# Two DMA issues of the first stage change queues: mixed outputs to ScalarE's, w_mod loads to GpSimd's

## The chip, the cores and the metric

The kernel is one program on one core of a Trainium2 chip. The metric is device time in microseconds (us), taken as the median of several runs. The core has five engines, each with an instruction queue of its own that runs in order: TensorE (PE, matmuls, with a separate queue for weight loads, PEld), VectorE (DVE), ScalarE (ACT), GpSimd (POOL) and SyncE (SP, which only issues DMAs). DMAs may be issued from SyncE's, ScalarE's and GpSimd's queues; 16 DMA engines carry them all. An instruction that has to wait for another engine holds everything behind it in its own queue.

## The reference

Two blocks run over 512 tokens of width 1024. The first block is an RWKV/GLA mixer followed by a routed expert layer. The second block has two layers, each a mixer followed by an expert-choice layer, and each modulated by vectors that come from a conditioning row:

```python
mix = jnp.concatenate([y_rw, y_gla], axis=-1)   # y_rw: rwkv7_mixer, y_gla: gla_mixer
x = x + mix @ w_out[l]
x = x + hier_moe(rmsnorm(x, ln2_w[l]), ...)
# second block, per layer l: 6 chunks of 1024
m = jax.nn.silu(c) @ w_mod[l] + b_mod[l]        # w_mod[l]: 1024 x 6144
sh1, sc1, g1, sh2, sc2, g2 = chunks of m
xl = xl + g1 * mixer(modulate(rmsnorm(xl), sh1, sc1))
xl = xl + g2 * ec_moe(modulate(rmsnorm(xl), sh2, sc2), ...)
```

The products with `w_mod` depend on the inputs alone, not on x, so they can run at any time before the second block needs them.

## The kernel before

Three stages follow each other: `phase1` with its expert layer `moe1`, `mixer0` with `moe2`, and `mixer1` with `moe2` again. The change touches `phase1`, the first 606 us.

`phase1` (line 238) norms and transposes x into `hT`. It then computes the recurrent half in four head pairs (`rwkv_pair`, line 359) and the GLA half in two (`gla`, line 620, a generator that yields between steps). Weights are loaded from SyncE's queue by `load` (line 248, DMA at line 251), each into one of two buffers of its kind (`w4` for w_rw; `wb` for w_gl, w_qk, w_v and w_og). Each of the eight 128-row slices of the mixed output is copied out of PSUM by ScalarE and stored to a DRAM buffer `ymix` by `mixed` (line 616), for the recurrent half as `t`, for the GLA half as `gt`. The next stage loads `ymix` again (`yin`, line 834) to multiply by w_out, whose pieces are loaded at line 774 (`st`).

The modulation is a filler. `adaln_block` (line 899) does one of 12 blocks (two layers, six chunks): eight loads of w_mod of 128 x 1024 (512 KB) into two buffers `wm`, four matmuls for each load into one bank `ad` (line 907). For the two gate chunks of a layer GpSimd loads four pieces of the bias `b_gate` (line 914), VectorE adds them (line 917), and GpSimd stores four pieces to `gates` (line 918). For the other chunks ScalarE copies the rows (line 920), TensorE turns them (line 923) and VectorE writes `mods` (line 931). GpSimd's queue also carries `nwr`, the norm weights of each GLA half (line 645), and at the stage's start some constants.

The code calls the fillers between the pairs:

```python
self.rwkv_pair(0, **X); gl(3); fill(6)
self.rwkv_pair(1, **X); gl(6); fill(2)
self.rwkv_pair(2, **X)
self.rwkv_pair(3, **X); fill(3); gl(99); fill(99)
```

This order is a priority, not the order on the chip: the framework plans the whole program when it is built, simulating engines and queues with costs of its own, and puts instructions on each queue as they become ready in that plan. It also adds all waits.

Of the kernel before, what the change touches and what calls it, by code (L numbers as in the profile page):

```python
# [20 lines left out]
T, D = 512, 1024  # L21
# [158 lines left out]
class Kern:  # L180
# [434 lines left out]

    def mixed(self, o, k, ps):
        self.nc.scalar.copy(o, ps)
        self.nc.sync.dma_start(self.ymix[k], o)

    def gla(self, P, bank, S, load, project, hT, gla_gw2, mask, keep, **_):  # L620
        nc, c, V, ident, A = self.nc, self.col, self.nc.vector, self.ident, self.A
# [277 lines left out]
    def adaln_block(self, l, j, w4, bank, row):  # L899

        nc, c = self.nc, self.col
        ps = bank()
        for k in range(KT):
            w = w4()
            nc.sync.dma_start(w, self.A["w_mod"][l, 128 * k:128 * k + 128, D * j:D * j + D])
            for g in range(4):
                nc.tensor.matmul(ps[32 * g:32 * g + 32, 0:256], self.sc[:, k], w[:, 256 * g:256 * g + 256], start=k == 0,  # L907
                                 stop=k == KT - 1, tile_position=(0, 32 * g))
        rows = row()
        if j in (2, 5):  # L910
            q = 2 * l + (j == 5)
            b = row()
            for g in range(4):
                nc.gpsimd.dma_start(b[32 * g:32 * g + 1], self.A["b_gate"][q:q + 1, 256 * g:256 * g + 256])
            for g in range(4):
                z = slice(32 * g, 32 * g + 1)
                nc.vector.tensor_add(rows[z], b[z], ps[z, 0:256])
                nc.gpsimd.dma_start(self.gates[q:q + 1, 256 * g:256 * g + 256], rows[z])
            return
        nc.scalar.copy(rows, ps[:, 0:256])  # L920
        ps = bank()[:, 0:16].rearrange("p (a g m) -> p a g m", a=2, m=2)
        for a in range(2):
            nc.tensor.matmul(ps[:, a], rows[:, 128 * a:128 * a + 128], self.sel, start=True, stop=True)

        where = {0: 1, 1: 0, 3: 3, 4: 2}[j] + 6 * l
        todo = [(where, 0)]
        if l == 0 and j < 2:
            todo.append((4 + (j == 0), 1))
        for slot, m in todo:
            o = self.mods[:, slot]  # L930
            nc.vector.tensor_add(o.rearrange("p (g a) -> p a g", a=2), ps[:, :, :, m],
                                 c(f"b_mod{l}{j}", 0, 8).rearrange("p (g a) -> p a g", a=2))
            if j in (1, 4):
                n = c(f"norm{1 if j == 1 else 2}_g_2{l}", 0, 8)
                nc.vector.scalar_tensor_tensor(o, o, 1.0, n, op0=OP.add, op1=OP.mult)
# [1093 lines left out]
```

## Time and profile before

| | |
|---|---|
| time, median of 3 runs | 2888.31 us (2879.37, 2888.31, 2890.34) |
| profiled execution | 2891.01 us, span of its trace 2889.4 us |
| granted TensorE clock, mean | 0.921 |
| TensorE busy | 2454.6 us (85%) |
| VectorE busy | 1124.1 us (39%) |
| ScalarE busy | 643.5 us (22%) |
| GpSimd busy | 107.0 us (4%) |
| moved by DMA | 778.42 MB, 269 GB/s |

The span is that of the trace; the execution's own time is a little longer. Busy shares are means over stages with different limits, so the first stage has to be read by itself. In the rows, `PE` is TensorE's matmuls and `PEld` its weight loads, `SPq`, `ACTq` and `POOLq` the DMA issues of a queue, `L907` a line of the kernel, and `ad<-wm,sc` a result with its operands. `out <- releaser` names a wait and what ended it.

### The profile page before, as it was taken

The page shows a single profiled execution, that of the slowest core. Times are in us where ns is not written, and L with a number is a line of the kernel's source. Part 1 is how long each engine was busy: PE and PEld are TensorE (multiplying, and loading weights), DVE is VectorE, ACT ScalarE, POOL GpSimd, SP SyncE. Part 2 cuts the span into 40 slices and gives each one's busy share as a digit, 9 for nine tenths or more (in the row PEclk, how much of TensorE's full clock was granted, in tenths as well). Part 3 has the DMA queues.
Part 4 walks back from the last instruction along what each step waited for, and adds up shares of the span by engine and source line. Part 5 has one row for each costly group of instructions (what it writes and reads, how often), then busy time and mean ns, then how long its engine had stood idle before and what let it go on. Part 6 is the DMA issues. An engine that isn't in the chain of part 4 may idle for free. (4 is left out here: it accounts for less than half of the span.)

```text
span 2889.4 us, 36529 instructions
## 1 busy us (share of the span) xinstructions
PE 2454.6 (85%) x15158; PEld 1352.8 (47%) x15158; DVE 1124.1 (39%) x2143; ACT 643.5 (22%) x1049; POOL 107.0 (4%) x193
## 2 busy tenths in 40 slices
PE   7999998775999988868889688988989669888897
PEld 3565655663534544436567433333347553333343
DVE  3867767534121320015875411111239641211112
ACT  3223313221102430005721200010034321000001
POOL 1000000001110000010000000000000000000000
PEclk9999998776999999988899798999999779999999
DMA  4355343056998999983133599999954259999996
GB/s 150 121 174 171 108 129 124 18 187 251 396 367 328 397 393 398 396 346 124 59 124 135 208 409 386 392 406 405 409 195 132 104 203 362 399 405 405 400 409 252
DMA packets 244551, 778.42 MB, mean 269 GB/s; under 512 B 15963, under 2 KB 17243, under 8 KB 243488
## 3 DMA queue, kind: packets, MB, share of 16 engines
q1 hardware_dynamic: 223616, 711.77, 65.2%
q0 software_dynamic: 12448, 41.50, 3.7%
q10 hardware_dynamic: 8320, 22.80, 2.2%
q8 instruction: 120, 1.97, 0.3%
q14 instruction: 47, 0.39, 0.0%
HBM read 748.73 MB, written 27.28 MB: 269 GB/s over the span
## 5 line engine op out<-in xcount | busy, mean ns | idle before, releaser
L1493 PE MATMUL G<-w,xT 128*64 128x256 f32 (+1 forms) x4096 | 772.4, 507 | 22.5 <-DMA w<-in_moe_w_up_dram 18.1
L1493 PEld LDWEIGHTS G<-w,xT 128*64 128x64 f32 x4096 | 293.1, 140 | 380.2 <-issue 287.6
L1513 PE MATMUL Y<-w,hT 128*64 128x512 f32 x1536 | 402.7, 602 | 2.6 <-DMA w<-in_moe_w_down_dram 1.3
L1513 PEld LDWEIGHTS Y<-w,hT 128*64 128x64 f32 x1536 | 172.2, 137 | 195.3 <-issue 182.6
L1498 DVE TENSOR_TENSOR h<-h,G 128x256 f32<-128x256 f32 (+1 forms) x64 | 35.4, 553 | 516.8 <-PE G L1493 406.8
L1761 DVE TENSOR_TENSOR xres<-xres,cb 128x512 f32<-128x512 f32 x116 | 79.6, 687 | 115.4 <-PE cb L1759 115.4
L1750 DVE SCALAR_TENSOR_TENSOR y<-Y,gate,g 128x512 f32<-128x512 f32 x32 | 24.0, 751 | 233.9 <-PE Y L1513 232.3
L321 PE MATMUL mm<-hT,w 128*128 128x512 f32 x240 | 113.2, 611 | 0.0
L1716 PE MATMUL gat<-ident,xg 128*128 128x128 f32 x128 | 30.4, 371 | 95.4 <-DMA xg<-xrow,tok 95.3
L1497 ACT ACTIVATE h<-G 128x256 f32<-128x256 f32 (+1 forms) x64 | 31.4, 491 | 343.3 <-PE G L1493 337.6
L1504 ACT COPY hT<-tr 128x256 f32<-128x256 f32 (+1 forms) x64 | 30.7, 479 | 274.8 <-PE tr L1503 274.8
L907 PE MATMUL ad<-wm,sc 128*32 128x256 f32 x768 | 70.5, 410 | 20.5 <-DMA wm<-in_w_mod_dram 19.1
L1209 PE MATMUL b<-big,wh 128*128 128x512 f32 x320 | 84.2, 415 | 4.4 <-ACT wh L854 3.0
L1751 ACT CAST yhi<-y 128x512 fp32r<-128x512 f32 x30 | 18.6, 619 | 310.5 <-DVE y L1750 224.2
L1716 PEld LDWEIGHTS gat<-ident,xg 128*128 128x128 f32 x128 | 19.1, 183 | 117.9 <-DMA xg<-xrow,tok 88.2
L1209 PEld LDWEIGHTS b<-big,wh 128*128 128x128 f32 x320 | 63.0, 199 | 22.6 <-ACT big L1190 5.4
L1759 PEld LDWEIGHTS cb<-yhi,ohT 128*128 128x128 f32 x114 | 21.4, 188 | 105.2 <-DVE xres L1761 56.8
L1503 PE MATMUL tr<-ident,h 128*128 128x128 f32 x192 | 35.8, 297 | 39.1 <-DVE h L1498 39.0
L636 PE MATMUL g<-wb,hT 128*64 128x128 f32 x1024 | 65.5, 276 | 3.3 <-DVE ga L711 2.6
L321 PEld LDWEIGHTS mm<-hT,w 128*128 128x128 f32 x240 | 42.9, 190 | 51.3 <-issue 50.3
L1759 PE MATMUL cb<-yhi,ohT 128*128 128x512 f32 x114 | 57.5, 504 | 9.7 <-ACT yhi L1751 9.7
L1711 POOL DMA_INDIRECT xg<-xrow,tok x32 | 31.1, 972 | 887.6 <-DVE tok L1793 435.7
(677 smaller groups left out, 3564.7 us busy)
## 6 DMA issues: line engine op xcount, KB each, us to landing
w<-in_exp_w_dram SPq DMA_DIRECT2D x384, 1024.0 KB, 13.2
w<-in_moe_w_gate_dram SPq DMA_DIRECT2D x64, 1024.0 KB, 15.6
w<-in_moe_w_up_dram SPq DMA_DIRECT2D x64, 1024.0 KB, 15.0
w<-in_moe_w_down_dram SPq DMA_DIRECT2D x64, 1024.0 KB, 15.3
wm<-in_w_mod_dram SPq DMA_DIRECT2D x96, 512.0 KB, 4.2
ws<-in_w_in_dram SPq DMA_DIRECT2D x20, 512.0 KB, 4.1
ws<-in_cf_w_dram SPq DMA_DIRECT2D x20, 512.0 KB, 3.5
st<-in_w_out_dram SPq DMA_DIRECT2D x16, 512.0 KB, 4.1
```

Source lines behind the costliest of these rows:

```text
L321: nc.tensor.matmul(ps[:m], w[:, k, col0:col0 + m], hT[:, k], start=k == 0, stop=k == KT - 1)
L636: nc.tensor.matmul(ps[half[h], b], hT[:, k, 64 * j:64 * j + 64], w[h][:, k], start=k == 0, stop=k == KT - 1)
L907: nc.tensor.matmul(ps[32 * g:32 * g + 32, 0:256], self.sc[:, k], w[:, 256 * g:256 * g + 256], start=k == 0, stop=k == KT - 1, tile_positio ...
L1209: nc.tensor.matmul(ps, a[:, k], b[:, k], start=m == 0 and k == 0, stop=m == 2 and k == KT - 1)
L1493: nc.tensor.matmul(parts[m][64 * c:64 * c + 64], xT[:, k, 64 * e:64 * e + 64], w[:, kk, H * c:H * c + H], start=k == 0, stop=k == KT - 1)
L1497: nc.scalar.activation(h, parts[0], AF.Silu)
L1498: nc.vector.tensor_mul(h, h, parts[1])
L1503: nc.tensor.transpose(ps[:, j].rearrange("p c s -> p (c s)"), h[:, 128 * j:128 * j + 128], self.ident)
L1513: nc.tensor.matmul(ys[n][64 * e:64 * e + 64], hTs[e][:, f], ws[e][:, ff_, 512 * n:512 * n + 512], start=f == 0, stop=f == nf - 1)
L1716: nc.tensor.transpose(ps[:, k], xg[:, 512 * b + 128 * k:512 * b + 128 * k + 128], self.ident[:m, :m])
L1759: nc.tensor.matmul(ps, ohT[:m, 128 * t:128 * t + 128], p[k][:m], start=k == 0, stop=k == 1)
L1761: V.tensor_add(xr, xr, ps)
```

## The change

The stores of `mixed` are issued from ScalarE's queue, behind the copy that fills them, and the loads of w_mod from GpSimd's queue. Both were on SyncE's. Sizes, buffers and the computation stay the same. `adaln_block` is called 12 times and `mixed` 8 times, all in the first stage.

```diff
@@ mixed
         self.nc.scalar.copy(o, ps)
-        self.nc.sync.dma_start(self.ymix[k], o)
+        self.nc.scalar.dma_start(self.ymix[k], o)
@@ adaln_block
             w = w4()
-            nc.sync.dma_start(w, self.A["w_mod"][l, 128 * k:128 * k + 128, D * j:D * j + D])
+            nc.gpsimd.dma_start(w, self.A["w_mod"][l, 128 * k:128 * k + 128, D * j:D * j + D])
```

## Rows read from the trace of the kernel before

**Rows 1.** The chain that ended last, its earliest long piece: start, us, what.
```profile
2651.80 0.95 DMA xg<-xrow,tok
```

**Rows 2.** Five stretches: length, busy PE, PEld, DVE, ACT, POOL (instructions), PEclk, DMA share, GB/s.
```profile
17.00:176.00 159.00, 153.77 (x1282) 84.56 (x1282) 96.44 (x189) 42.82 (x70) 1.97 (x4) 1.00 0.36 117
176.00:275.00 99.00, 89.56 (x972) 49.07 (x964) 76.76 (x150) 33.68 (x54) 5.78 (x12) 0.97 0.63 200
275.00:440.00 165.00, 160.61 (x2120) 109.32 (x2120) 112.18 (x244) 49.90 (x87) 4.93 (x10) 0.98 0.37 117
440.00:512.00 72.00, 54.70 (x628) 38.58 (x626) 59.40 (x123) 26.15 (x41) 1.92 (x4) 0.82 0.36 118
512.00:606.00 94.00, 66.74 (x1040) 59.90 (x1040) 39.81 (x90) 18.04 (x31) 1.95 (x4) 0.74 0.03 9
```

**Rows 3.** TensorE's waits, 17.3:440 and 440:607: us in total, times, longest.
```profile
PE ad L907 <- DMA wm<-in_w_mod_dram: 8.5, 12, 1.3
...
PE ad L907 <- DMA wm<-in_w_mod_dram: 10.6, 7, 3.8
```

**Rows 4.** Waits of TensorE's weight loads, 17:606.
```profile
PEld ad L907 <- DMA wm<-in_w_mod_dram: 34.9, 32, 4.3
```

**Rows 5.** Lines L905, L877, L918: duration in ns, min/median/max.
```profile
L905 SPq DMA_DIRECT2D wm<-in_w_mod_dram x96: 327/328/1899, 6.0 to 504.4; - x96
...
L877 POOL DMA_DIRECT2D xrow<-w x12: 533/546/616, 649.9 to 2350.6; - x12
...
L918 POOL DMA_DIRECT2D gates<-rows x16: 487/487/487, 184.5 to 525.0; - x16
```

**Rows 6.** Waits at the head of SyncE's queue, 0:640.
```profile
SPq L905 <- PE ad L907: 202.9, 79, 30.4
```

**Rows 7.** Timeline of SyncE's queue, 484:512: start, us, instruction.
```profile
487.10 0.80 SPq L251 DMA_DIRECT2D wb<-in_w_og_dram  x2
489.70 15.01 SPq L905 DMA_DIRECT2D wm<-in_w_mod_dram  x6
```

**Rows 8.** Timelines of ScalarE and SyncE at the stage's end, 604:611.
```profile
604.20 0.59 ACT L617 COPY gt<-g 128x512 f32<-128x512 f32 x1 [3.76 <-PE g L763]
607.22 0.41 ACTq L1213 DMA_DIRECT2D lnrow<-in_ln_row_dram  x1
...
604.81 0.32 SPq L618 DMA_DIRECT2D ymix<-gt  x1
```

**Rows 9.** DMA issues by line: count, KB each, median us to landing.
```profile
wm<-in_w_mod_dram SPq DMA_DIRECT2D x96, 512.0 KB, 4.2
...
xrow<-w POOLq DMA_DIRECT2D x12, 512.0 KB, 3.0
...
out_dram<-o SPq DMA_DIRECT2D x4, 512.0 KB, 2.7
...
rw_w<-in_rw_w_dram POOLq DMA_DIRECT2D x1, 256.0 KB, 6.1
...
nwr<-in_gla_nw_dram POOLq DMA_DIRECT2D x4, 32.0 KB, 6.9
```

**Rows 10.** Timeline of TensorE, 17:26.
```profile
21.06 1.06 PE L907 MATMUL ad<-wm,sc 128*32 128x256 f32 x2
```

**Rows 11.** The page's costliest groups: busy, mean ns, idle before.
```profile
L907 PE MATMUL ad<-wm,sc 128*32 128x256 f32 x768 | 70.5, 410 | 20.5 <-DMA wm<-in_w_mod_dram 19.1
```

**Rows 12.** Waits of GpSimd's queue, 0:640.
```profile
POOL gates L918 <- DVE rows L917: 254.4, 7, 75.6
...
POOL nwr L645 <- DVE ga L756: 69.5, 1, 69.5
```

**Rows 13.** Timeline of GpSimd, 510:526, the first and last of four.
```profile
513.57 0.49 POOL L918 DMA_DIRECT2D gates<-rows  x1 [69.00 <-DVE rows L917]
...
525.05 0.49 POOL L918 DMA_DIRECT2D gates<-rows  x1 [0.69 <-DVE rows L917]
```

**Rows 14.** Groups of VectorE, 17:606: busy, mean ns.
```profile
L411 DVE TENSOR_TENSOR t<-t,k 128x512 f32<-128x512 f32 x8 | 5.5, 685 | 0.0
```

## The prediction

> **What bounds the kernel now.** The time before is 2888.3 us (median of three, 2879.4 to 2890.3). The profiled execution took 2891.0 us, its trace spans 2889.4 us, so the sum below is made against 2891.0 and 2.7 us are taken off at the end. A measurement of this kernel can tell about 0.5% (14 us) from no change.
>
> I read the chain that ended last first. Its pieces lie in the expert layers near the end of the span [rows 1], and it is silent on the first stage, which runs to about 606 us. For an earlier stage the question is whether its own last instruction comes earlier; the engines' busy time in stretches answers that. From 17 to 176 us and from 275 to 440 us TensorE is busy 153.77 of 159 and 160.61 of 165 us: matmuls, in their order, are the bound. From 176 to 275 us it is busy 89.56 of 99. From 440 to 512 us VectorE is the fuller one (59.40 of 72 us against 54.70), and after 512 us neither is full: dependences between engines set the pace [rows 2]. TensorE runs its instructions in order, so where it is full a late operand pushes back all the rest; where it is not, a late operand can be swallowed.
>
> Then the waits that the change can touch. TensorE's matmul queue waited for a w_mod load 12 times before 440 us, 8.5 us in all, and 7 times after, 10.6 us in all [rows 3]: 19.1 us. Its weight-load queue shows 32 such waits, 34.9 us, most of them beside running matmuls [rows 4]. No engine's list of waits names another load of SyncE's line in this stretch. So 19.1 us, 0.66% of the time, is all that a better w_mod feed can give back directly, and the 8.5 us are the surer part.
>
> **SyncE's side.** It sheds 96 loads at 0.328 us of issue [rows 5], 31 us of queue time, and eight stores. SyncE's line often stands still with a w_mod load at its head, 202.9 us waiting for TensorE to free one of the two buffers [rows 6], and at times with a store there. Neither costs the kernel anything now, because the loads behind them are not missed by anyone. Gone, they free nobody: 0. What can gain is a w_mod load that stands behind another load. The clearest place is 487.10 us, where two w_og loads go out right before the w_mod loads of 489.70 us [rows 7], and the longest wait of TensorE for such a load, 3.8 us [rows 3], falls there. A line of its own would send that load earlier, though the same data engines would still carry three transfers. I take 4 us for all such places; the bounds are 0 and the whole 19.1 us.
>
> **ScalarE's side.** It gains eight issues. A DMA issued from its queue took 0.41 us; the store that SyncE issues now starts at 604.81 us, when the copy (604.20 plus 0.59) has just ended [rows 8]. So a store holds ScalarE for about 0.4 us, eight for 3.3 us, on an engine busy 171 of 589 us [rows 2], which hides them. If all lay on the path they would cost 3.3 us; the last one lies there, and against SyncE's 0.32 us it costs 0.1 us. I take 0.5 us. Behind the last store stand the first issues of the next stage, which wait for its landing anyway.
>
> **GpSimd's side: the turnaround.** With two buffers, load k+2 can go out only when TensorE has read load k. So the dense stretch from 176 us on is paced by the turnaround: buffer free, issue, landing (median 4.2 us [rows 9]). What GpSimd adds to a 512 KB load isn't in this trace; the nearest rows are its 512 KB stores of xrow. They take 0.546 us to issue against SyncE's 0.328 [rows 5] and land in 3.0 us against 2.7 us for SyncE's 512 KB output stores [rows 9]. Depending on whether landing already holds the issue, a turnaround grows by 0.3 us or by 0.5 us. Loads from GpSimd's line show more: nwr landed in 6.9 us and the 256 KB of rw_w in 6.1 us [rows 9], but nwr is made of 512-byte rows, and rw_w went out among the first nine loads of SyncE. I take 0.3, from the row with the same size and row length. On the 19 waits of the matmul queue that is 5.7 us. Upper bound: 6.9 in place of 4.2 us on all 19, 51 us. Below zero I see no reason, since both lines feed the same data engines.
>
> **GpSimd's side: its line.** 96 issues of 0.55 us are 53 us on an engine busy 17 us in 589 [rows 2]; there is room. But the line is in order, and the loads now share it with the gate blocks: four groups of four tiny b_gate loads, four groups of four gate stores at 0.487 us each [rows 5], 1.95 us a group. A w_mod load caught behind a group is that much later. Five of the eight groups lie in or beside the stretches in which TensorE waits for loads now; I take 1 us for three of them, 3 us. Bounds: 0, and 8 times 1.95, 16 us.
>
> The rows of the gate stores also weigh a rule. Their issue is 0.487 us from the shortest to the longest [rows 5], while VectorE is busy two thirds of the time: no issue was held by VectorE. The Trainium skill, "SBUF — State Buffer", section "SBUF: two separate sides" (its "DVE blocks DMA" box), says that GpSimd cannot write DMA descriptors while VectorE runs an operation in a two-port mode, and puts such a transfer at about 3.1 us in place of 0.62. By that figure, 19 exposed loads would lose 2.5 us each, 47 us, for a time of about 2938 us, an estimate from that page. By the row it is 0. The stores measured are of one row each, so a load of 128 rows isn't settled by them; its case stands below as a rival, priced from rows.
>
> **The sum.** 0 + 0.5 + 5.7 + 3 - 4 = +5 us: 2896 us as profiled, 2893 us against the median. The terms' own bounds reach from -19 us to +70 us (3.3 + 51 + 16).
>
> **What the sum can't hold: the order.** The instructions aren't in the order of the code. w_mod matmuls run at 21.06 us [rows 10], before the first recurrent pair, though the code asks for them after it: a planner lays out every queue when the program is built. Moving 96 loads to another queue moves w_mod blocks and all that is packed around them. That can pull either way, and is in the first two rivals.
>
> **Rivals.**
> *Faster: the feed stops stalling TensorE, and blocks slide to where it is idle.* For: a load on its own line can go out as soon as its buffer is free, and TensorE has 17 us and 27 us idle after 440 and 512 us [rows 2]. A w_mod load costs TensorE 70.5 us / 96 = 0.73 us [rows 11]; the last load goes out at 504.4 us [rows 5], 100 us before the stage ends, so blocks may slide. All 19.1 us of waits gone gives 2869 us; ten loads sliding out of the full stretches give 7 us more, 2862. Against: in the dense stretch the loads wait for buffers, not for the queue, and a new queue has no more buffers. Time: 2866 us.
> *Slower: GpSimd's line blocks.* A w_mod load that the planner put behind a gate store waits until VectorE has added the bias, and VectorE runs late. GpSimd stood 254.4 us waiting for VectorE before gate stores and 69.5 us before the nwr load [rows 12], harmless today since nothing stood behind. The last four gate stores went out one by one from 513.57 to 525.05 us [rows 13], 12 us in place of 2. If two blocks in the full stretches do that with loads behind, the cost is 2 x 10 us; with the turnaround's 5.7 us that is 2914 us. It decides from the point where TensorE waits longer than the 3.8 us of today for one load. Against: the planner knows the wait and may put the next two loads ahead of it.
> *Slower: GpSimd's loads land late.* If they land as rw_w did, 1.9 us later than now, the 19 waits grow by 36 us: with the sum's other terms about 2923 us. One way to it is VectorE holding the issue: half an operation (0.685 us for a 512-wide one [rows 14]) for the 65% of the time that VectorE is busy is 0.22 us a load, on 19 to 96 loads 4 to 21 us, 2897 to 2914 us. I put the case at 2915. Against: the flat 0.487 us, and the 3.0 us of the xrow stores.
> *The change does nothing, because buffers and not queues pace the loads,* is the ground of the forecast itself and has no time of its own.
>
> **Numbers.** Forecast (2879 to 2902 us) 0.46; faster rival 0.26; blocked line 0.19; late landing 0.09. Faster by over 0.5% (below 2874): 0.25; within 0.5%: 0.48, which takes a little of each rival; slower (above 2903): 0.27. The range runs from the faster rival's 2862 us to 2922 us, past both slower rivals' times; what lies beyond, towards the sum's upper bound, is less than 2 in 10.
>
> **What would show it.** Right: TensorE's waits for w_mod loads in the first stage stay within 12 to 35 us, w_mod issues from GpSimd at about 0.55 us, landing within 0.5 us of 4.2, the stage ends within 10 us of 606. SyncE's heads shrink and nobody notices. ScalarE's stores start within 0.1 us of their copies' ends. Wrong: landings above 6 us or issues of uneven length (late landing, VectorE's hold); a single wait over 4 us with GpSimd stopped before a gate store or nwr (the blocked line); waits gone, or the first stage ending more than 15 us early with w_mod matmuls past 510 us (the slide). A stage end that moves with w_mod waits unchanged would say that the new order, not the queue's speed, made the difference.

## The result, and the profile after

The changed kernel takes 2912.59 us (median of 8 runs, 2902.82 to 2919.68) against 2889.39 us for the kernel before (8 runs beside it): ratio 1.0078, 95% interval 1.0059 to 1.0097. Measured again beside the experiments it gave 1.0072 (1.0059 to 1.0085). It is slower by about 22 us, 0.75%, where +5 us was forecast as the likeliest. The time lies inside the forecast range. It is also near the 2914 us of the rival in which GpSimd's line blocks, but it came about in another way: that nearness is luck.

The profiled execution spans 2911.5 us. Its five stretches, to be held against [rows 2] (the same columns: length, busy PE, PEld, DVE, ACT, POOL, PEclk, DMA share, GB/s):

```profile
17.00:176.00 159.00, 153.09 (x1238) 83.88 (x1240) 96.49 (x189) 41.33 (x67) 12.54 (x24) 0.99 0.36 115
176.00:275.00 99.00, 85.46 (x872) 46.47 (x872) 71.93 (x142) 29.87 (x48) 22.81 (x44) 0.98 0.63 197
275.00:440.00 165.00, 156.08 (x2101) 105.69 (x2102) 110.79 (x242) 49.96 (x86) 17.96 (x34) 0.96 0.33 106
440.00:512.00 72.00, 58.52 (x692) 41.87 (x687) 56.37 (x118) 25.78 (x44) 10.40 (x20) 0.84 0.39 126
512.00:606.00 94.00, 68.28 (x1106) 57.34 (x1106) 44.94 (x101) 18.72 (x31) 3.01 (x6) 0.74 0.07 23
```

TensorE is 4 us less busy from 176 to 275 us and 4.5 us less from 275 to 440 us: it stands still in the very stretches that it paces. What it stands for is in the lists of waits, matmul queue and weight-load queue, 17 to 640 us (us in total, times, longest; before: [rows 3, 4]):

```profile
PE ad L907 <- DMA wm<-in_w_mod_dram: 33.7, 28, 6.5
...
PEld ad L907 <- DMA wm<-in_w_mod_dram: 54.7, 43, 6.9
```

The waits for w_mod loads went from 19.1 to 33.7 us. The loads themselves, on GpSimd's line (duration ns min/median/max; then what GpSimd waited for ahead of them; then the landing, and the row of the DMA issues that answers to [rows 9]):

```profile
L905 POOL DMA_DIRECT2D wm<-in_w_mod_dram x96: 527/527/560, 11.5 to 518.8; - x96
...
  PE ad L907: 409.1, 73
  DMA wm<-in_w_mod_dram: 22.7, 7
  issue: 6.3, 2
...
DMA to landing us min/median/max: 4.0/4.4/9.2
```

```profile
wm<-in_w_mod_dram POOLq DMA_DIRECT2D x96, 512.0 KB, 4.4
```

ScalarE's last two copies and the stores behind them (start, us; before: [rows 8]). A store starts 0.03 us after its copy has ended, and the last store of the stage starts at 620.95 us where SyncE's started at 604.81:

```profile
615.99 0.58 ACT L617 COPY gt<-g 128x512 f32<-128x512 f32 x1 [6.58 <-PE g L763]
616.60 0.33 ACTq L618 DMA_DIRECT2D ymix<-gt  x1
620.33 0.58 ACT L617 COPY gt<-g 128x512 f32<-128x512 f32 x1 [3.76 <-PE g L763]
620.95 0.33 ACTq L618 DMA_DIRECT2D ymix<-gt  x1
```

So the first stage ends 16.1 us later. Comparing the starts of the same TensorE instructions in both traces, the lag is 8 us by 290 us, 12 by 365, 16.6 by 530; it then stays at 13 to 16.5 us through the whole of the middle, and grows once more, from 16.4 to 23.3 us, between 2430 and 2693 us, in the last expert section, where no instruction of TensorE stands in another order than before. Two losses have to be explained: 16 us in the stage that was changed, and 7 us in one that wasn't.

One place in the first stage is plain to see. GpSimd's line and TensorE's matmuls around 500 us (idle before the instruction, and its releaser, in brackets):

```profile
496.34 1.46 POOL L914 DMA_DIRECT2D rows<-in_b_gate_dram  x3
503.84 1.07 POOL L905 DMA_DIRECT2D wm<-in_w_mod_dram  x2 [6.04 <-issue]
504.90 0.50 POOL L914 DMA_DIRECT2D rows<-in_b_gate_dram  x1
```

```profile
507.99 1.08 PE L907 MATMUL ad<-wm,sc 128*32 128x256 f32 x8 [6.46 <-DMA wm<-in_w_mod_dram]
509.26 1.08 PE L907 MATMUL ad<-wm,sc 128*32 128x256 f32 x8 [0.19 <-DMA wm<-in_w_mod_dram]
513.65 1.06 PE L907 MATMUL ad<-wm,sc 128*32 128x256 f32 x2 [3.31 <-DMA wm<-in_w_mod_dram]
```

Two w_mod loads stand in the middle of a group of four b_gate loads, GpSimd idles 6.04 us ahead of them for something that the profile does not name, and TensorE waits 6.46 us. TensorE had read the first load's buffer 3.26 us before that load went out; nearly half of the 6.46 us is therefore the line, and the rest is the issue and the landing, as in the 3.8 us of before at the same matmuls.

The rest needs experiments, because three things changed at once: the queue of the loads, the queue of the stores, and the planner's order of nearly everything in the stage (some 3200 of TensorE's matmuls in it stand at another place in the order).

### The profile page after: what moved, and what is told of

The parts are those of the page before. It is cut to its first block, busy times and chain, and to the rows that moved or that the text cites. A ratio compares the mean times of both kernels' runs of the same rounds, so it can differ in the third digit from the quotient of the medians.

```text
span 2911.5 us, 36526 instructions
## 1 busy us (share of the span) xinstructions
PE 2467.0 (85%) x15158; PEld 1356.7 (47%) x15158; DVE 1123.5 (39%) x2143; ACT 642.8 (22%) x1049; POOL 157.6 (5%) x289
## 5 line engine op out<-in xcount | busy, mean ns | idle before, releaser
L1497 ACT ACTIVATE h<-G 128x256 f32<-128x256 f32 (+1 forms) x64 | 31.4, 490 | 350.5 <-PE G L1493 350.5
L907 PE MATMUL ad<-wm,sc 128*32 128x256 f32 x768 | 71.1, 415 | 34.1 <-DMA wm<-in_w_mod_dram 33.7
L905 POOL DMA_DIRECT2D wm<-in_w_mod_dram x96 | 50.9, 532 | 441.0 <-PE ad L907 409.1
## 6 DMA issues: line engine op xcount, KB each, us to landing
w<-in_moe_w_down_dram SPq DMA_DIRECT2D x64, 1024.0 KB, 16.1
```

What stands on the lines that cost most here:

```text
L905: nc.gpsimd.dma_start(w, self.A["w_mod"][l, 128 * k:128 * k + 128, D * j:D * j + D])
L1497: nc.scalar.activation(h, parts[0], AF.Silu)
```

## Experiments

Each was measured beside the kernel before; the ratio is to it. "Stage end" is the start of the last first-stage copy (L617) in its profile, 604.2 us before, 620.3 after. "Half clock" is the time up to there in which TensorE's granted clock was at 1.2 in place of 2.4 GHz, counted from the trace: 87 us before, 104 after. Both come from one execution each, which lies up to 9 us from its kernel's median (2915.2 beside 2905.9 us for "after, order of before"); the ratio is from all of them.

| kernel | median us | ratio (95%) | waits for w_mod | half clock | stage end |
|---|---|---|---|---|---|
| before | 2886.5 | | 19.1 | 87 | 604.2 |
| after, first and again | 2912.6, 2908.4 | 1.0078, 1.0072 | 33.7, 31.4 | 104, 98 | 620.3, 620.2 |
| after, order of before | 2905.9 | 1.0059 (1.0037-1.0082) | 36.8 | 108 | 623.0 |
| before, order of after | 2895.9 | 1.0025 (1.0008-1.0041) | 21.1 | 84 | 605.4 |
| stores on ScalarE alone | 2900.5 | 1.0038 (1.0019-1.0056) | 19.5 | 117 | 617.5 |
| the same, order of before | 2889.2 | 1.0013 (1.0002-1.0024) | 20.9 | 87 | 603.3 |
| after, gate DMAs on SyncE | 2907.2 | 1.0065 (1.0039-1.0090) | 28.9 | 87 | 614.1 |
| every second load on GpSimd, order of before | 2909.8 | 1.0072 (1.0049-1.0095) | 29.8 | 110 | 620.9 |
| w_mod on ScalarE, order of before | 2901.6 | 1.0051 (1.0033-1.0070) | 23.1 | 83 | 610.8 |
| before, four shared buffers | 2901.5 | 1.0044 (1.0029-1.0059) | 5.5 | 124 | 613.7 |
| after, four shared buffers, the same order | 2902.5 | 1.0049 (1.0033-1.0065) | 11.1 | 142 | 622.8 |
| before, loads in column halves, order of before | 2883.1 | 0.9986 (0.9973-0.9998) | 9.0 | 77 | 598.2 |
| before, last store made late | 2901.2 | 1.0050 (1.0031-1.0068) | 19.4 | 87 | 601.0 |

**Queue against order, both ways.** The order of TensorE's, VectorE's and ScalarE's instructions in the first stage is written into the kernel as a list and tied with edges that force issue order but make nobody wait. So the changed queues can run in the old order, and the old queues in the new order.

```
     with tile.TileContext(nc) as tc:
         Kern(nc, tc, A, out[0], at).build()
+        keep_order(nc, tc)     # for p, q in pairs of the list:
+                               #     tc.add_manual_dep(q, p, NoSync)
```

After, in the order of before:

> The changed kernel, with TensorE's, VectorE's and ScalarE's first-stage instructions held in the order of the kernel before (the queues stay as changed). Theory A, GpSimd's turnaround: the buffer-to-landed time stays about 0.4 us longer than on SyncE and TensorE's waits for w_mod loads stay at 30 us or more; first stage ends about 12 to 18 us later than before, the whole is 12 to 20 us slower than before (2901 to 2909). Rival B, the new planned order: the waits fall back to about 19 us and the time to within 5 us of before (2889). Rival C, ScalarE's stores: as A, but the waits for w_mod stay near 19 us.

```profile
PE ad L907 <- DMA wm<-in_w_mod_dram: 36.8, 29, 6.8
...
PEld ad L907 <- DMA wm<-in_w_mod_dram: 57.2, 43, 7.3
```

Before, in the order of after:

> The kernel before (all on SyncE), with TensorE's, VectorE's and ScalarE's first-stage instructions held in the order of the changed kernel. Theory A, turnaround: within 6 us of before, waits for w_mod loads about 19 to 24 us. Rival B, order: slower than before by 14 to 22 us (2903 to 2911), with the first stage ending near 621 us, and more exposed loads than 19. Rival C, stores: no change.

```profile
PE ad L907 <- DMA wm<-in_w_mod_dram: 21.1, 23, 3.9
...
PEld ad L907 <- DMA wm<-in_w_mod_dram: 43.2, 40, 4.4
```

The queues carry most of the loss. With the old order the new queues still cost 17 to 19 us and the waits stay at 36.8 us; with the new order the old queues end the stage 1.2 us late and wait 21.1 us. The new order's own price over the whole run, 1.0025, is about 7 us (2 to 12), at the edge of what can be told.

**The stores alone,** free and in the old order.

```
     def mixed(self, o, k, ps):
         self.nc.scalar.copy(o, ps)
-        self.nc.sync.dma_start(self.ymix[k], o)
+        self.nc.scalar.dma_start(self.ymix[k], o)
```

> Only the eight stores move to ScalarE; w_mod stays on SyncE; the planner is free. Theory A: within 5 us of before (2884 to 2894). Rival B, order: its order differs from that of before too, so it may move by some us either way, with w_mod waits moving along. Rival C, stores: slower by 15 us or more.

It was 1.0038 slower, which my theory had at nothing, with the waits for w_mod where they were. So the same edit was run in the order of before:

> Only the eight stores move to ScalarE, and TensorE, VectorE and ScalarE keep the order of before. Theory: within 4 us of before (2883 to 2891), the first stage ends within 2 us of before, time at the half clock in the stage about the same: then the 11 us that the free-order kernel lost were its order's. Rival: the stores themselves cost, 8 us or more slower, and a wait behind ScalarE's issues shows up.

Most of the loss went (1.0013, stage end 603.3). Eight stores on ScalarE cost 0.6 to 7 us at most; the planner's order that came with them cost more. So the queue that carries the loss of the changed kernel is that of the w_mod loads. Two stretches of each show what the order cost. The kernel whose order was free first, then the one in the old order (length, busy PE, PEld, DVE, ACT, POOL, PEclk, DMA share, GB/s):

```profile
176.00:275.00 99.00, 90.97 (x894) 50.62 (x894) 75.94 (x149) 30.68 (x49) 5.75 (x12) 0.91 0.66 205
275.00:440.00 165.00, 158.56 (x2032) 107.10 (x2034) 106.67 (x234) 47.76 (x83) 4.91 (x10) 0.94 0.31 99
```

```profile
176.00:275.00 99.00, 89.13 (x983) 48.61 (x977) 76.75 (x150) 33.83 (x55) 5.78 (x12) 0.98 0.65 201
275.00:440.00 165.00, 160.67 (x2116) 108.76 (x2113) 112.90 (x244) 50.69 (x87) 4.93 (x10) 0.98 0.37 116
```

TensorE is about as busy, and gets less done: 894 matmuls in place of 983 in the first of the two, at a granted clock of 0.91 in place of 0.98. (The counts are a rough measure, since with another order other matmuls stand in the same stretch.) The plainest place is from 200 to 220 us, free and in the old order:

```profile
200.00:220.00 20.00, 19.23 (x161) 13.76 (x161) 9.46 (x16) 1.71 (x4) 1.91 (x4) 0.66 0.48 150
```

```profile
200.00:220.00 20.00, 17.24 (x212) 12.13 (x212) 13.32 (x22) 2.06 (x5) 1.92 (x4) 1.00 0.65 192
```

Over the stage it stood at 1.2 GHz for 117.3 us in place of 86.6; half of the 31 us is 15, and the stage ended 14.2 us later. A share of busy time does not show such a loss; the clock's column does. In the free kernel the clock fell at 203.2 us and stayed down for 13.7 us. What TensorE had waited for ahead of that place, in the free kernel and in the old order:

```profile
200.71 0.64 PE L907 MATMUL ad<-wm,sc 128*32 128x256 f32 x8 [1.23 <-DMA wm<-in_w_mod_dram]
```

```profile
200.31 0.64 PE L907 MATMUL ad<-wm,sc 128*32 128x256 f32 x8 [2.10 <-DMA wm<-in_w_mod_dram]
```

The longer wait of the two was followed by no fall. Why one order loses the clock and the other doesn't stays open.

**GpSimd's line cleared of the gate DMAs.** TensorE, VectorE and ScalarE keep the changed kernel's order here without being tied.

```
-                nc.gpsimd.dma_start(b[32 * g:32 * g + 1], self.A["b_gate"]...)
+                nc.sync.dma_start(b[32 * g:32 * g + 1], self.A["b_gate"]...)
...
-                nc.gpsimd.dma_start(self.gates[...], rows[z])
+                nc.sync.dma_start(self.gates[...], rows[z])
```

> The changed kernel with the b_gate loads and the gate stores on SyncE, so that GpSimd's line carries little but w_mod loads; the order of TensorE, VectorE and ScalarE is the same as in the changed kernel. Theory A: faster than the changed kernel by 3 to 8 us only (the 6.5 us wait near 508 us and the 3.3 us one go, the 0.4 us a load stay): 2905 to 2910. Rival D, GpSimd's line blocks (w_mod loads stand behind gate groups): faster by 12 us or more, close to before.

```profile
PE ad L907 <- DMA wm<-in_w_mod_dram: 28.9, 27, 3.9
...
PEld ad L907 <- DMA wm<-in_w_mod_dram: 54.3, 45, 4.7
```

The 6.5 us wait is gone (longest 3.9) and the stage ends 6 us sooner than after, but 10 us are left, with as many waits. The median, 2907.2, can't be told from the changed kernel's, and the profiled execution, 2900.8 us, is one of the fastest of this kernel. The blocked line is at most a part of the loss.

**Is it the turnaround?** If so, more buffers ahead should hide it. In the changed kernel and in the kernel before, w_mod loads and the gated layer's weight loads share four buffers in place of two and two:

```
-                t = P([128, 1024], "wb" if back else "w4", bufs=2)
+                t = P([128, 1024], "wb" if back else "w4", bufs=4 if back else 2)
...
-            fills = (self.adaln_block(l, j, lambda: P([128, 1024], "wm", bufs=2), ...
+            fills = (self.adaln_block(l, j, lambda: P([128, 1024], "wb", bufs=4), ...
```

> The kernel before with w_mod loads and the gated layer's weight loads sharing four buffers in place of two and two; all on SyncE, planner free. If buffers and turnaround pace the loads, most of the 19 us of waits for w_mod go and the stage ends 5 to 20 us earlier, unless the shared ring makes the loads wait for each other or the new order loses clock. Rival: the waits stay, then the landing and not the buffers set them.

> The changed kernel with the four shared buffers, TensorE, VectorE and ScalarE in the order of the four-buffer kernel that keeps all on SyncE (2901.5, waits for w_mod 5.5 us). Theory: with two more buffers ahead the 0.4 us of turnaround are hidden; waits 5 to 9 us and within 6 us of that kernel, where with two buffers the same change cost 17 to 23 us. Rival, GpSimd's line itself costs: again 15 us or more slower than it (2916 or more).

Before's, then after's waits:

```profile
PE ad L907 <- DMA wb<-in_w_mod_dram: 5.5, 7, 1.6
```

```profile
PE ad L907 <- DMA wb<-in_w_mod_dram: 11.1, 12, 2.6
```

With two buffers the move costs some 20 us; with four it costs 0.05% (1.0049 beside 1.0044), and with both intervals no more than 8 us. The waits are a third of those with two buffers, though at 11.1 us over the 9 expected, and in the single profile the stage does end 9 us later. That most of the loss goes with two more buffers fits the turnaround; that a part stays possible is left standing. The four-buffer kernels are slower than before all the same, against my expectation: the waits went and the stage still ended later, with 124 us at the half clock in place of 87. Whether the new order or the shared buffers cost that clock is not shown, since four buffers were not run in the order of before.

**A dose.** Every second load on GpSimd, the rest and the stores on SyncE, in the order of before.

```
-            nc.sync.dma_start(w, self.A["w_mod"]...)
+            (nc.gpsimd if k % 2 else nc.sync).dma_start(w, self.A["w_mod"]...)
```

> Every second w_mod load (odd k) goes out from GpSimd, the others and the stores from SyncE, in the order of before. Theory, turnaround per load: TensorE's waits for w_mod between those of before and those with all loads on GpSimd, about 24 to 30 us, and half of the loss or so, 5 to 12 us slower. Rival, a shared line decides (standing behind other loads or gate groups): with two lines no load waits behind another, so no slower than before, or faster.

```profile
wm<-in_w_mod_dram SPq DMA_DIRECT2D x48, 512.0 KB
wm<-in_w_mod_dram POOLq DMA_DIRECT2D x48, 512.0 KB, 4.8
```

A miss: waits of 29.8 us as forecast, but the whole loss, not half. At the first recurrent copy, 182 us, the kernel was 7.5 us late already. The loads themselves do not tell why. The 4.8 us of the row hold 29 of GpSimd's 48 loads and none of SyncE's; counted from the completions of all 96 loads in the trace, SyncE's landed in 4.1 us and GpSimd's in 4.65 (medians), where 96 loads from one line took 4.2 before and 4.45 after. And each line issued as it does alone, 0.06 and 0.33 us after the buffer came free. The Trainium skill, "DMA: Bandwidth & Descriptors", section "SWDGE vs HWDGE vs iDMA", says that each data engine takes turns between the queues of the two kinds; no run here shows the turns. The stage's time at the half clock, 110 us, is as long as with all loads on GpSimd. So the loss does not scale with the number of slow loads, and what made half of them cost the whole stays open.

**Away from SyncE, but not to GpSimd.**

```
-            nc.sync.dma_start(w, self.A["w_mod"]...)
+            nc.scalar.dma_start(w, self.A["w_mod"]...)
```

> w_mod loads leave SyncE for ScalarE's queue (stores stay on SyncE); TensorE's, VectorE's and ScalarE's own work keep the order of before. Theory, GpSimd's slower turnaround is the cost: where ScalarE is idle a load goes out some 0.06 us after its buffer is free and lands as from SyncE (4.2 us); it loses only where ScalarE is in an activation, so waits for w_mod 19 to 27 us and a time within 10 us of before, well under the 17 to 23 us that GpSimd's line cost. Rival, any queue but SyncE's costs (w_mod away from the loads beside which it was planned): slower by 15 us or more.

```profile
PE ad L907 <- DMA wm<-in_w_mod_dram: 23.1, 24, 4.8
...
wm<-in_w_mod_dram ACTq DMA_DIRECT2D x96, 512.0 KB, 4.4
```

Waits as forecast, the stage 6.6 us late, the median 15 us (1.0033 to 1.0070), which is more than my bound of 10. The waits lie far below GpSimd's 36.8 us in the same order, but the times of the two can't be told apart (GpSimd's 1.0037 to 1.0082), so the rival in which any queue but SyncE's costs is not ruled out. ScalarE's line has a price of its own. A w_mod load that waits for its buffer holds ScalarE's work behind it: outside the copies of the modulation (L920) ScalarE waited 29 us in this kernel for TensorE to read w_mod, in the kernel before not at all. How much of the 15 us that makes is not shown. The longest group of these waits:

```profile
ACT L682 <- PE ad L907: 8.7, 2, 5.0
```

**Smaller pieces.** Each load cut into two column halves, four buffers of half the size, on SyncE, in the order of before.

```
+            for g in range(4):
+                if g % 2 == 0:
+                    w = w4()     # [128, 512], bufs=4
+                    nc.sync.dma_start(w, self.A["w_mod"][l, 128 * k:128 * k + 128,
+                                      D * j + 256 * g:D * j + 256 * g + 512])
```

> The kernel before with each w_mod load cut into two column halves (256 KB) in four buffers of half the size, on SyncE, in the order of before: a half's buffer is free two matmuls earlier. Theory, the turnaround sets the waits: smaller loads land sooner, waits 10 to 18 us, 0 to 8 us faster than before. Rival, the data engines set them (bytes in flight are the same, 192 loads and rows of 2 KB): 19 us or more, same or slower.

```profile
PE ad L908 <- DMA wm<-in_w_mod_dram: 9.0, 6, 4.1
...
wm<-in_w_mod_dram SPq DMA_DIRECT2D x192, 256.0 KB, 3.7
```

The waits fell to 9.0 us and the stage ends 6 us sooner than before. At 2883.1 us, 0.9986 (0.9973 to 0.9998), it is the one version that beats both kernels, by little.

**The later loss.** The changed kernel once more, and the kernel before with nothing but a late end of the stage:

```
+        for _ in range(3 if k == 7 else 0):
+            self.nc.sync.dma_start(self.ymix[k], o)
+            self.nc.sync.dma_start(o, self.ymix[k])
         self.nc.sync.dma_start(self.ymix[k], o)
```

> The changed kernel once more, beside the others. Theory: 1.006 to 1.010 of before. Its profile also tells whether the 6.8 us that the first profile of it lost between 2450 and 2720 us (where no instruction's order differs) come back: if they are the change's they are there again, if they are that execution's they are not.

> The kernel before with three store-and-load round trips ahead of its last mixed store, so that the second stage starts some 13 to 20 us late and nothing else differs (the queues and the order are those of before). It tells what a mere delay does to the later stages. If the changed kernel's later loss (half-clock stretches in the expert section, 6.8 us) comes from its lateness, the profile's last expert section (2351 to 2717 us before, 365.8 us) takes some 372 us here too; if it comes from the first stage's instructions, 366 us and the loss is the delay alone.

One stretch of the last expert section (columns as above), before, after, after again, and before made late:

```profile
2440.00:2720.00 280.00, 244.69 (x1062) 97.64 (x1061) 53.93 (x95) 26.89 (x56) 4.74 (x5) 0.95 1.02 404
```

```profile
2440.00:2720.00 280.00, 246.03 (x1040) 97.77 (x1036) 48.55 (x85) 25.48 (x54) 4.71 (x5) 0.92 1.00 394
```

```profile
2440.00:2720.00 280.00, 245.52 (x1039) 97.59 (x1036) 48.99 (x86) 25.70 (x54) 4.74 (x5) 0.92 1.00 394
```

```profile
2440.00:2720.00 280.00, 245.54 (x1057) 97.28 (x1054) 56.35 (x98) 27.48 (x57) 4.71 (x5) 0.95 1.02 404
```

The loss came back: the clock is 0.92 again where before has 0.95. In the trace the falls to 1.2 GHz stand at the same places, after waits for gathered rows; between 2460 and 2690 us of before, and over the same instructions after, they add up to 23.9 and 37.5 us, and half of the 13.6 us is the 6.8 us lost. The four profiles with a lag of 15.6 us or more at 2430 us have it (after, after again, after in the old order, every second load); of the others four lose about 3 us (the changed kernel with four buffers, 15.0 us late, but also the column halves, 6 us early), and the rest nothing. A lag of 13.2 us with all loads on SyncE (the stores' kernel) and one of 9.4 us with the loads on GpSimd (gate DMAs on SyncE) did not bring it. The kernel made late tells less than it was meant to: it was 3 us early when its round trips began, 10 us late at 700 us and 7.5 us late at 2430 us, so a lag of 16 us was not tried without the loads. What sets the length of these stretches stays open.

## Why the prediction held in its range and missed in its likeliest case

- **What bounds the stage.** Right: TensorE in order, in the dense stretches, paced by the turnaround of two buffers. The four-buffer pair and the column halves support it; that half of the loads on GpSimd cost the whole loss does not follow from it.
- **SyncE's side, the relief of 4 us.** Wrong: there was nothing to relieve. In the trace of before every load from the third on, 94 of them, went out 0.05 to 0.08 us after TensorE had read its buffer, that of 489.70 us behind the two w_og loads as well. None stood behind another load, and the 3.8 us wait there was the turnaround itself: that load landed 4.1 us after its issue.
- **ScalarE's side, 0.5 us.** Right within the measurement: stage end 0.9 us earlier, the whole 1.0013 (1.0002 to 1.0024), 0.6 to 7 us.
- **The turnaround, 5.7 us: the term that was too small.** It was 0.3 us a load times the 19 loads that TensorE waited for. The 0.3 was right. From the buffer's release to the issue a load takes 0.33 us on GpSimd and 0.06 on SyncE, counted from both traces; landing medians were 4.2 to 4.5 us on either line in the profiles that use one line and two buffers. The 19 was wrong. With the gate DMAs out of the way the waits rose by 9.8 us, of which the new order by itself brings 2.0 (21.1 us on the old queues); 7.8 to 9.8 us over 0.27 are 29 to 36 loads, not 19. They could have been counted in the trace of before: of the 96 loads, 30 were used by a matmul that started within 0.3 us of their landing, that is, with no room for 0.3 us more, and 30 x 0.27 = 8.1 us. A load that lands just in time shows no wait in the list of matmuls, and is as exposed as one that does. The list of weight loads in [rows 4] had nearly the same number, 32 waits, which the prediction set aside because matmuls ran beside them.
- **GpSimd's line, 3 us.** The gate DMAs did cost, but twice as much and in another form: 6 us lie between the stage ends of after and of the kernel with the gate DMAs on SyncE, 5 of them arising between 440 and 530 us, where GpSimd idled 6.04 us. The half clock differs in this pair too (104 and 87 us), so the 6 us are not the line's alone.
- **What the sum lacked: the clock.** The stage's time at the half clock grew by 11 to 21 us in the three profiles of the changed queues (after, again, old order), and the last expert section lost 6.8 us that way. No term stood for it. The sum with what the runs showed is 0 + 0 + 10 + 6 + 0 = 16 us for the stage, of which the clock is not a separate part that could be taken out, and 6.8 us behind it: 22.8 us, against 22.1 us between the two spans. The 10 and the 6 are differences of stage ends, so they meet the 16 by construction; how much of each is waits and how much is clock is not shown.
- **The order.** It could pull either way, as the prediction said, but it wasn't what decided here: +1.2 us at the stage's end for the new order on the old queues. That an order can cost more than half as much as the queues did, the stores' kernel shows (11 us).
- **The rivals.** Landing late fell (4.4 us). The Trainium skill's rule that GpSimd can't write descriptors while VectorE works in a two-port mode ("SBUF — State Buffer", section "SBUF: two separate sides") did not show here: 96 loads of 128 rows took 527 to 560 ns to issue while VectorE was busy 380 of 589 us. The blocked line came in another form than told: a b_gate group and a wait for nothing named, in place of a gate store that waits for VectorE. The faster rival had nothing for it: the column halves show that the feed can be improved (9.0 us of waits), but on SyncE's line, with smaller loads and four buffers.

By its own signs the prediction said that waits of 12 to 35 us and a stage end within 10 us go together. The waits came to 33.7 us, inside, and the stage ended 16 us late: the two bounds did not fit each other.

## What to carry to other kernels

Where loads are paced by a short ring of buffers, a slower issue costs every load that lands just in time, not only those that are waited for today: count loads whose first reader starts within the added delay of their landing. Give such loads a line with a fast issue and with no work behind them that could be held up, and check first whether they stand behind anything at all: here they went out as soon as their buffer was free. Smaller pieces gained a little; four shared buffers took the waits away and lost more at the clock. And when an edit lets a planner order the work anew, run the edit once in the old order: here the same eight stores cost 11 us with a new order and some 4 us (0.6 to 7) with the old one.

## What the runs showed of the hardware

- TensorE's granted clock fell to 1.2 GHz for short stretches in a part of the stage where TensorE was busy 91 of 99 us (granted 0.91, the stores' kernel), at 203.2 us after a wait of 1.23 us; a wait of 2.10 us at the same place in the old order was followed by no fall. Which order of the same matmuls ran made 117.3 us of the first stage in place of 86.6, some 14 us of time.
- A 512 KB load whose buffer comes free goes out 0.06 us later from SyncE's line (before) and from ScalarE's when that is idle, 0.33 us later from GpSimd's (after). These are medians, from the end of the last matmul that reads the buffer.
- Loads from two lines in turn landed in 4.1 us (SyncE's) and 4.65 us (GpSimd's), where loads of one line took 4.2 and 4.45.
- The profile puts 7 waits of GpSimd, 22.7 us, down to an earlier w_mod load that had to land. Each of these seven loads went out 0.31 to 0.33 us after TensorE had read its buffer, as the others did, so it was the buffer that they waited for. SyncE's list in the kernel before has the same kind of wait, without a later issue:

```profile
SPq L905 <- DMA wm<-in_w_mod_dram: 91.7, 51, 12.5
```
